# Twenty-four input-projection blocks as plain fp32 matmuls on a scaled copy of x

## The chip, the cores and the metric

The kernel runs on one core of a Trainium2 chip. The metric is the device time of one execution in microseconds (us). Three runs of the kernel before took 1295.62, 1296.11 and 1300.11 us, median 1296.11. Engines are named as in the profile: PE is TensorE (matmul; PEld its weight loads), DVE is VectorE, ACT is ScalarE, POOL is GpSimd, SP is SyncE, which here only issues DMAs.

## The reference

One encoder layer on 272 tokens (16 meta tokens and 256 of the input), width 2048, all in float32. RMSNorm of the input times `g` goes through one large projection W_in. Its columns are the input of an S5 state-space mixer (1024), queries and keys (1024), values (1024), output gates o (1024) and 32 gate values. Then two mixers run side by side, their outputs go through W_out, and a convolution-gated feed-forward part follows.

```
h  = h + W_out [ norm(S5(u)) || mLSTM(q, k, v, o, gates) ],   [u|qk|v|o|gates] = RMSNorm(h) W_in
h  = h + (silu(conv(hn W_gate)) * (hn W_up)) W_down,           hn = RMSNorm(h)
qk = silu(dwconv(qk_in));   y_ml = sigmoid(o_pre) * norm(mLSTM)
S5: y = gelu(scan_fwd(u) + scan_bwd(u) + d*u);  y * sigmoid(y W_glu + b)
```

## The kernel before

Activations stand with the channels on the 128 partitions and the 272 tokens along the free axis. Weights are streamed from DRAM in halves of 128x1024 (512 KB). A product has to be as good as float32: each half is split into a high part `hi` (ScalarE, L241) and a remainder `lo` (VectorE, L242) of the fast fp32r type, with three buffers each for `raw`, `hi` and `lo` (`piece`, from L236). `mm3` then does three matmuls per 128x128 weight tile (L257 to L259): hi times Xh, hi times Xl, lo times Xh, where Xh and Xl are x times g, split in the same way at the start (`split`, L279 and L280). A window block (`win_block`) is 128 columns of W_in: 16 weight tiles, two halves, 48 matmuls. There are 33 of them: one for the gate values, u0 to u7 for S5, qk0 to qk7 (of which qk0 to qk3 are the queries and need 258 columns only), v0 to v7, and o0 to o7 (258 columns). Each is emptied by VectorE, which multiplies by the token's factor R = 1/rms (L497, L638, L662, L681).

The S5 mixer has a chain of its own, on VectorE and GpSimd:
- tables of powers (`s5_tables`), of which one goes to DRAM (`td`, L375, two DMAs) and comes back spread over the partitions (`tcf`, L514);
- input coefficients for 16 half-blocks (L527 to L530), each followed by small matmuls, the in-projection (L543), into the state tile ST;
- a recurrence in three parts: `rec_local` (six steps of L551 to L554, first product on VectorE, second on GpSimd), `rec_carry` (15 steps of four small VectorE operations, L573 to L576), `rec_spread` (six steps in two halves, with the last sum on GpSimd);
- output coefficients for m = 0 to 7 (`s5_coefs`; zz L825 to L827 and c2 L834 on GpSimd, c1 L833 and L835 on VectorE), matmuls with them (L845, L860), a sum on VectorE that ends each m (L867), and a last matmul (L892);
- the GLU: a product with W_glu (L257 on `yg`) and a sigmoid (L925).

The mLSTM follows (L699 is one of its plain fp32 matmuls), then W_out and the feed-forward part.

The order of instructions on each engine is set when the program is built: a scheduler of the framework simulates the code and places each instruction where its simulated time and priority put it. `hp()` raises the priority of the code inside it; `behind` keeps one instruction behind another. In the code the blocks o, qk and v come after S5, but the scheduler puts them among S5's matmuls, where TensorE would wait. Tiles come from pools that stand at fixed places of SBUF on a left and a right side; a ring is a tag with a number of buffers that are used in turn.

Of the kernel before, what the change touches and what calls it, by code (L numbers as in the profile page):

```python
# [9 lines left out]
F32 = mybir.dt.float32  # L10
# [6 lines left out]
P = 128  # L17
# [4 lines left out]
KD = D // P  # L22
# [138 lines left out]
def body(ctx: ExitStack, tc: tile.TileContext, A: dict, out: bass.AP, dbg: dict = {}):  # L161
# [23 lines left out]
    def ring(p, tag, bufs):  # L185
        return lambda name, shape=(P, L), dt=F32: p.tile(list(shape), dt, tag=tag, bufs=bufs, name=name)

    l4 = ring(lq, "l4", 8)
    r1m = ring(lq, "r1m", 4)
    r1g = ring(lq, "r1g", 6)  # L190


    ST = ls.tile([P, 64, 2, C], F32, name="ST")
    STf = ST.rearrange("p a r c -> p (a r c)")
    e_li, li = pool("li")
    a4 = ring(li, "a4", 2)
    s2 = ring(li, "s2", 2)
# [94 lines left out]
    xcs = []  # L292

    def x_load(q, a=0, b=4):
        if a == 0:
            xcs.append(l4("xc", [P, 4, L]))
        return nc.sync.dma_start(xcs[q][:, a:b], A["xt"][:, 4 * q + a:4 * q + b, :])

    def x_split(q, a=0, b=4):
# [5 lines left out]
    def s5_tables():  # L305
# [66 lines left out]
            S.copy(tkc[0:64, 3 - i], t[0:64, :, 64:128])  # L372
            S.copy(tkc[64:128, i], t[64:128, :, 64:128])
        for d in range(2):
            nc.sync.dma_start(td[:, :, :, d].rearrange("s g j r p -> (g j) s (r p)"),  # L375
                              tkc[64 * d:64 * d + 64].rearrange("x s r p -> x s (r p)"))
        cmul(lam[2], l1, l1, 0, 64, G, w2, w3)
        cmul(lam[3], lam[2], l1, 0, 64, G, w2, w3)
# [42 lines left out]
    with hp():  # L421
        x_load(0, 0, 2)
        nc.sync.dma_start(vec, A["vec"])
        nc.sync.dma_start(par, A["par"])
        pieces = [piece(w0[:, :1024], CUTS)]
        x_split(0, 0, 2)
        x_load(0, 2)
        x_split(0, 2)
        x_load(1)
        x_split(1)  # L430
        pieces.append(piece(w0[:, 1024:], [1024]))
        for q in (2, 3):
            xd = x_load(q)
            x_split(q)
        get0 = getter(pieces)
        for q in range(4):
            S.activation(xcs[q], xcs[q], AF.Square)
            if q:
                (V if q == 3 else G).tensor_tensor(out=xcs[0], in0=xcs[0], in1=xcs[q], op=ALU.add)
# [3 lines left out]
    def X(t0, t1):  # L443
        return lambda i: (Xh[:, i, t0:t1], Xl[:, i, t0:t1])

    def win_block(b, t0=0):
        get = get0 if b == 0 else stream(A["win"][b], KD)
        p = bank("mm")
        mm3(p[:, :L - t0], get, X(t0, L), KD)
        return p  # L450

    pg = win_block(0)
    gsb = r1g("gsb")
    acc = bank("acc")
    tb = s5_tables()
    for j in range(4):
        nc.tensor.matmul(acc[:, :L], ones, xcs[0][:, j, :], start=(j == 0), stop=(j == 3))
    with hp():
        rstd(R, acc[:, :L], 1.0 / D)
    with hp():  # L460
# [5 lines left out]
    q_sb = l4("q_sb", [P, 4, N])
    kE = l4("kE", [P, 4, L])
    kO = l4("kO", [P, 4, L])
    osb = [l4("osb", [P, 4, N]) for _ in range(2)]
    for o in (*osb, q_sb):  # L470
        G.memset(o[:, 0, 0:1], 0.0)
    G.memset(kE[64:128], 0.0)
    G.memset(kO[0:64], 0.0)

# [153 lines left out]

    def qk_block(m):
        t0 = T0 if m < 4 else 0
        p = win_block(9 + m, t0)
        x = r1m("qx", [P, L + 2])
        G.memset(x[:, t0:t0 + 1], 0.0)
        G.memset(x[:, L + 1:L + 2], 0.0)
        with hp():
            V.tensor_tensor(out=x[:, t0 + 1:L + 1], in0=p[:, :L - t0], in1=R[:, t0:], op=ALU.mult)  # L638
        t = r1m("qt")
        tt = t[:, t0:]  # L640
        S.activation(tt, x[:, t0 + 1:L + 1], AF.Identity, scale=vc("qw", 8 + m), bias=vc("qb", m))
        with hp():
            V.scalar_tensor_tensor(out=tt, in0=x[:, t0:L], scalar=vc("qw", m), in1=tt, op0=ALU.mult, op1=ALU.add)
            V.scalar_tensor_tensor(out=tt, in0=x[:, t0 + 2:L + 2], scalar=vc("qw", 16 + m), in1=tt, op0=ALU.mult, op1=ALU.add)
        if m < 4:
            S.activation(q_sb[:, m, :], t[:, T0:], AF.Silu)
        else:
            S.activation(kE[0:64, m - 4, :], t[0:64], AF.Silu)
            S.activation(kO[64:128, m - 4, :], t[64:128], AF.Silu)

    Vt = [None, None, None]
    vm = lq.tile([P, 8, META], F32, name="vm")
    vmt = lq.tile([P, P], F32, name="vmt")

    def v_block(h):
        if h == 0:
            for i in range(3):
                Vt[i] = l4(f"V{i}", [P, 8, P])
        p = win_block(17 + h)
        vt = r1m("vt")  # L660
        with hp():
            V.tensor_tensor(out=vt, in0=p[:, :L], in1=R, op=ALU.mult)  # L662
# [284 lines left out]
    for m in range(8):  # L947
        u_block(m)
        if m < 4:
            behind(nc.sync.dma_start(bts[m], A["bt"][m]), last_raw[0])  # L950
        if m >= 1:
            s5_in(m - 1)
        if m == 4:
            G.memset(ST[:, 32:64, :, 0:1], 0.0)
    s5_in(7)
    rec_local(tb, 0)
    rec_local(tb, 1)
# [46 lines left out]
    nc.sync.dma_start(ch, A["cst"][:, NC0:])

# [135 lines left out]
```

## Time and profile before

| | us |
|---|---|
| median of three runs | 1296.11 |
| the profiled execution | 1294.34 |
| its span (first to last instruction) | 1292.6 |
| PE busy | 1225.7 (95%) |
| DVE busy | 874.2 (68%) |
| ACT busy | 603.8 (47%) |
| POOL busy | 369.6 (29%) |
| mean granted clock of TensorE | 0.972 |

Times in the rows below count from the span's start. A matmul's row gives its start and its length; matmuls overlap, so the distance from start to start is what one costs. A row "[2.49 <-DMA x]" says that the engine stood idle for 2.49 us before the instruction and what ended that. The parts of the program stand in the trace as follows: gate and u blocks up to 61 us, input coefficients to 115, `rec_local` to 176, `rec_carry` to 217, `rec_spread` to 273, output coefficients to 328, the last v blocks to 357, then the GLU.

### The profile page before, as it was taken

Reading aid. Unit: us, or ns where it says so; the run is one execution under the profiler, and the core shown is the slowest. Engines: PE = TensorE matmul, PEld = TensorE weight load, DVE = VectorE, ACT = ScalarE, POOL = GpSimd, SP = SyncE. Lnnn points to the kernel's source line nnn. Section 1 sums busy time; section 2 is a strip of 40 time slices with the busy share of each in tenths; the row PEclk is TensorE's granted clock in tenths of the full one; section 3 lists DMA queues with packets and bytes.
Section 4 is the critical chain, followed back from the end, with each engine's and each line's share of the span. In section 5 each row is a group of like instructions: output and inputs, shape, how many; then the busy total and the mean of one; then the engine's idle time right before and its main releaser. Section 6 shows DMA issues by size and latency. Waiting matters only on the chain.

```text
span 1292.6 us, 23440 instructions
## 1 busy us (share of the span) xinstructions
PE 1225.7 (95%) x9393; PEld 1126.8 (87%) x9393; DVE 874.2 (68%) x1083; ACT 603.8 (47%) x922; POOL 369.6 (29%) x428
## 2 busy tenths in 40 slices
PE   6889898898999999999999999999999999999995
PEld 5878898777998779999999998888999999998885
DVE  7779999973465488766666665555666666665554
ACT  7734244322476345544444444334444444445552
POOL 4476822685035363221111110000111111120111
PEclk8989899789999999999999999999999999999998
DMA  6777454343574355556556556666656656566663
GB/s 246 221 228 211 137 165 155 123 114 96 142 232 131 97 183 171 185 183 184 187 185 184 186 186 181 194 192 188 192 182 187 186 184 189 182 177 191 193 192 111
DMA packets 90753, 227.88 MB, mean 176 GB/s; under 512 B 21052, under 2 KB 36884, under 8 KB 90644
## 3 DMA queue, kind: packets, MB, share of 16 engines
q1 hardware_dynamic: 83924, 224.21, 57.0%
q10 hardware_dynamic: 6720, 2.16, 0.7%
q8 instruction: 74, 1.21, 0.4%
q14 instruction: 35, 0.29, 0.1%
HBM read 219.81 MB, written 5.48 MB: 174 GB/s over the span
## 4 chain that ended last, share of the span: by engine, by line
PE 75%; DVE 11%; DMA 4%; issue 4%; ACT 3%; POOL 1%; ACTq 1%; SPq 0%; DVEq 0%; POOLq 0%
PE ps_mm L268 25%; PE ps_mm L269 13%; PE ps_mm L257 10%; PE ps_mm L258 10%; PE ps_mm L259 10%; DVE lo L242 3%; PE ps_s L543 1%; ACTq L878 1%; DVE t L551 1%; PE ps_acc L845 1%; DVE ST L553 1%; PE ps_s L259 1%; PE ps_s L258 1%; PE ps_s L257 1%; ACT hi L241 1%
## 5 line engine op out<-in xcount | busy, mean ns | idle before, releaser
L242 DVE TENSOR_TENSOR lo<-raw,hi 128x1024 fp32r<-128x1024 f32 (+2 forms) x379 | 486.5, 1284 | 244.6 <-ACT hi L241 244.0
L241 ACT ACTIVATE hi<-raw 128x1024 fp32r<-128x1024 f32 (+2 forms) x379 | 393.8, 1039 | 461.0 <-PE ps_mm L268 202.4
L268 PE MATMUL ps_mm<-X,hi 128*128 128x512 f32 x704 | 249.8, 398 | 0.0
L268 PE MATMUL ps_mm<-a,hi 128*128 128x512 f32 x704 | 244.2, 390 | 0.0
L258 PE MATMUL ps_mm<-X,hi 128*128 128x258 f32 x704 | 199.6, 284 | 0.0
L1081 POOL TENSOR_TENSOR gt<-gt,R 128x256 f32<-128x256 f32 x44 | 59.5, 1352 | 487.1 <-ACT gt L1080 487.1
L257 PE MATMUL ps_mm<-X,hi 128*128 128x258 f32 x704 | 198.6, 282 | 0.0
L269 PE MATMUL ps_mm<-a,lo 128*128 128x256 f32 x704 | 198.5, 282 | 0.0
L259 PE MATMUL ps_mm<-X,lo 128*128 128x258 f32 x704 | 197.7, 281 | 0.0
L269 PE MATMUL ps_mm<-X,lo 128*128 128x256 f32 x704 | 197.0, 280 | 0.0
L259 PE MATMUL ps_mm<-Xh,lo 128*128 128x272 f32 (+1 forms) x528 | 161.9, 307 | 11.3 <-DVE lo L242 11.1
L257 PE MATMUL ps_mm<-Xh,hi 128*128 128x272 f32 (+1 forms) x528 | 160.5, 304 | 10.1 <-ACT hi L241 8.2
L258 PE MATMUL ps_mm<-Xl,hi 128*128 128x272 f32 (+1 forms) x528 | 159.2, 302 | 1.3 <-DVE Xl L280 1.3
L268 PEld LDWEIGHTS ps_mm<-X,hi 128*128 128x128 f32 x704 | 132.3, 188 | 29.5
L268 PEld LDWEIGHTS ps_mm<-a,hi 128*128 128x128 f32 x704 | 132.2, 188 | 27.7
L257 PEld LDWEIGHTS ps_mm<-X,hi 128*128 128x128 f32 x704 | 132.3, 188 | 2.2
L259 PEld LDWEIGHTS ps_mm<-X,lo 128*128 128x128 f32 x704 | 134.2, 191 | 0.0
L269 PEld LDWEIGHTS ps_mm<-X,lo 128*128 128x128 f32 x704 | 133.8, 190 | 0.0
L258 PEld LDWEIGHTS ps_mm<-X,hi 128*128 128x128 f32 x704 | 133.3, 189 | 0.0
L269 PEld LDWEIGHTS ps_mm<-a,lo 128*128 128x128 f32 x704 | 133.1, 189 | 0.0
L259 PEld LDWEIGHTS ps_mm<-Xh,lo 128*128 128x128 f32 x528 | 107.1, 203 | 15.2 <-DVE lo L242 14.0
L257 PEld LDWEIGHTS ps_mm<-Xh,hi 128*128 128x128 f32 x528 | 106.9, 203 | 12.3 <-ACT hi L241 8.5
(326 smaller groups left out, 1818.0 us busy)
## 6 DMA issues: line engine op xcount, KB each, us to landing
raw<-wg SPq DMA_DIRECT2D x88, 512.0 KB
raw<-wu SPq DMA_DIRECT2D x88, 512.0 KB, 4.4
raw<-win SPq DMA_DIRECT2D x65, 512.0 KB, 3.7
raw<-wd SPq DMA_DIRECT2D x64, 512.0 KB, 3.6
raw<-wout SPq DMA_DIRECT2D x32, 512.0 KB, 4.3
raw<-wd SPq DMA_DIRECT2D x32, 384.0 KB, 3.8
tcf<-td SPq DMA_DIRECT2D x16, 256.0 KB, 4.2
bc<-bcs SPq DMA_DIRECT2D x16, 256.0 KB, 3.4
```

The lines of the kernel that those rows point to most:

```text
L241: S.activation(hi[:, a:b], raw[:, a:b], AF.Copy)
L242: V.tensor_tensor(out=lo[:, a:b], in0=raw[:, a:b], in1=hi.bitcast(F32)[:, a:b], op=ALU.subtract)
L257: nc.tensor.matmul(out_ap, h, xh, start=(first and i == 0), stop=False)
L258: nc.tensor.matmul(out_ap, h, xl, start=False, stop=False)
L259: nc.tensor.matmul(out_ap, l, xh, start=False, stop=(last and i == n - 1))
L268: nc.tensor.matmul(both[:, :, :cols], h, x, start=(i == 0), stop=False)
L269: nc.tensor.matmul(both[:, 1, :cols], l, x[:, 0, :], start=False, stop=(i == n - 1))
L543: nc.tensor.matmul(pv[gg, d, ri, :], ic[gg, q, d, ri, :], uj[gg], start=True, stop=True)
L551: V.tensor_tensor(out=t1, in0=src, in1=lr[:, sl].unsqueeze(2).unsqueeze(3).to_broadcast([P, 32, 2, n]), op=ALU.mult)
L553: V.tensor_tensor(out=dst, in0=dst, in1=t1, op=ALU.add)
L845: mk_ = nc.tensor.matmul(kp[32 * g:32 * g + 32, 112 * qq + c0:112 * qq + c0 + 64], zf[gg, 16 * w:16 * w + 32], c1[gg, w].rearrange("p h k ...
L1081: G.tensor_tensor(out=t, in0=t, in1=R2[:, 2:], op=ALU.mult)
```

## The change

A new tile X holds x in float32 for the whole first part. After u0 VectorE multiplies it by g_mix and R in place, in 16 operations. The 24 blocks o, qk and v take their weights as they come from DRAM (`whole`) and multiply them as float32 with X (`win_plain`), one matmul call per weight tile where there were three. The three buffers of `raw`, `hi` and `lo` each serve in turn for such halves. Since R is in X already, ScalarE empties the blocks: the sigmoid of o is taken straight from PSUM, and `o_gates` goes away. The o and qk blocks use the PSUM banks of two tags in turn. The tiles osb, q_sb, kE, kO and V move to a pool of their own that opens where Xh and Xl end, the ring l4 goes from 8 buffers to 4 in another pool, the squares of x get tiles of their own, and h1 takes the place of X later. The S5 tables are built at high priority, and the two `td` stores are issued by ScalarE.

```diff
+    hx = ctx.enter_context(tc.tile_pool(name="hx", bufs=1, side="left"))
-    l4 = ring(lq, "l4", 8)
+    l4 = ring(ls, "l4", 4)
+    X = hx.tile([P, KD, L], F32, tag="h1", name="X")
+    xcs = [X[:, 4 * q:4 * q + 4, :] for q in range(4)]
...
-            nc.sync.dma_start(td[:, :, :, d].rearrange("s g j r p -> (g j) s (r p)"),
+            nc.scalar.dma_start(td[:, :, :, d].rearrange("s g j r p -> (g j) s (r p)"),
...
+    def whole(src):
+        tag = ("raw", "hi", "lo")[plain[0] % 3]
+        plain[0] += 1
+        w = st.tile([P, 1024], F32, tag=tag, bufs=3, name="wf")
+        nc.sync.dma_start(w, src)
+        return w
+
+    def win_plain(b, t0=0, tag="mm"):
+        p = bank(tag)
+        with hp():
+            w = [whole(A["win"][b][:, 1024 * j:1024 * j + 1024]) for j in range(2)]
+        for k in range(KD):
+            nc.tensor.matmul(p[:, :L - t0], w[k // 8][:, k % 8 * P:k % 8 * P + P], X[:, k, t0:],
+                             start=(k == 0), stop=(k == KD - 1))
+        return p
...
-    tb = s5_tables()
+    with hp():
+        tb = s5_tables()
...
-        p = win_block(9 + m, t0)
+        p = win_plain(9 + m, t0, ("mm", "ml")[m % 2])
-            V.tensor_tensor(out=x[:, t0 + 1:L + 1], in0=p[:, :L - t0], in1=R[:, t0:], op=ALU.mult)
-        S.activation(tt, x[:, t0 + 1:L + 1], AF.Identity, scale=vc("qw", 8 + m), bias=vc("qb", m))
+            S.copy(x[:, t0 + 1:L + 1], p[:, :L - t0])
+            S.activation(tt, p[:, :L - t0], AF.Identity, scale=vc("qw", 8 + m), bias=vc("qb", m))
...
-        p = win_block(17 + h)
+        p = win_plain(17 + h)
-            V.tensor_tensor(out=vt, in0=p[:, :L], in1=R, op=ALU.mult)
+            S.copy(vt, p[:, :L])
...
-        p = win_block(25 + h, T0)
-        o = osb[h // 4][:, h % 4, :]
-            V.tensor_tensor(out=o, in0=p[:, :N], in1=R[:, T0:], op=ALU.mult)
-    def o_gates():
-        for o in osb:
-            S.activation(o, o, AF.Sigmoid)
+        p = win_plain(25 + h, T0, ("mm", "ml")[h % 2])
+            S.activation(osb[h // 4][:, h % 4, :], p[:, :N], AF.Sigmoid)
...
+        if m == 0:
+            for k in range(KD):
+                V.scalar_tensor_tensor(out=X[:, k, :], in0=X[:, k, :], scalar=vc("g_mix", k), in1=R, op0=ALU.mult, op1=ALU.mult)
```

The change moves instructions in three places that matter below. The line numbers of the kernel after are up to 12 higher than those of the kernel before.

On SP before, the two stores of the table (td, from the tile tkc) stood among the loads of weight halves (raw):

```order
L375 DMA td<-tkc 64x4x128
L240 DMA raw<-win 128x1024
L375 DMA td<-tkc 64x4x128
L240 DMA raw<-win 128x1024
L624 DMA cmd<-gc 8x16 x2
L514 DMA tcf<-td 64x1x1024 x2
```

On ScalarE after, they stand among its hi parts and copies; un is the tile of a u block's columns:

```order
L242 ACTIVATE hi<-raw 128x1024
L514 COPY un<-un 128x4x16
L515 COPY un<-un 128x4x16
L373 COPY tkc<-ST 64x128
L374 COPY tkc<-ST 64x128
L376 DMA td<-tkc 64x4x128
L242 ACTIVATE hi<-raw 128x1024
L376 DMA td<-tkc 64x4x128
```

The second store now comes behind a hi, which is that of the second half of u5.

On VectorE before, at the start of the spread (t and ST are the recurrence's products and sums, qx and qt belong to the convolution of qk), lo parts stood between the steps:

```order
L242 TENSOR_TENSOR lo<-raw,hi 128x1024
L551 TENSOR_TENSOR t_1488<-ST,l4r 128x1024
L551 TENSOR_TENSOR t_1494<-ST,l8r 128x1024
L643 SCALAR_TENSOR_TENSOR qt<-qx,vec,qt 128x272
L553 TENSOR_TENSOR ST<-ST,t_1488 128x64x16
L242 TENSOR_TENSOR lo<-raw,hi 128x1024
L553 TENSOR_TENSOR ST<-ST,t_1494 128x64x16
L644 SCALAR_TENSOR_TENSOR qt<-qx,vec,qt 128x272
L638 TENSOR_TENSOR qx<-ps_mm,R 128x272
L242 TENSOR_TENSOR lo<-raw,hi 128x1024
L551 TENSOR_TENSOR t_1500<-ST,l12r 128x1024
```

On VectorE after, the same place:

```order
L562 TENSOR_TENSOR t_1513<-ST,l4r 128x1024
L562 TENSOR_TENSOR t_1519<-ST,l8r 128x1024
L564 TENSOR_TENSOR ST<-ST,t_1513 128x64x16
L564 TENSOR_TENSOR ST<-ST,t_1519 128x64x16
L562 TENSOR_TENSOR t_1525<-ST,l12r 128x1024
L564 TENSOR_TENSOR ST<-ST,t_1525 128x64x16
L562 TENSOR_TENSOR t_1531<-ST,l4r 128x1024
```

The steps follow each other, with no lo and no eviction between them.

On TensorE before, the matmuls of the output coefficients (ST times c, into ps_s) had matmuls of a v block on both sides, and others up to the end of S5:

```order
L257 MATMUL ps_mm<-Xh,hi 128x272
L860 MATMUL ps_s_1529<-ST,c_1536 64x68 x16
L860 MATMUL ps_s_1529<-ST,c_1579 64x68
L667 MATMUL ps_ml<-cst,vt 128x128 x2
L860 MATMUL ps_s_1529<-ST,c_1579 64x68 x15
L258 MATMUL ps_mm<-Xl,hi 128x272
L259 MATMUL ps_mm<-Xh,lo 128x272
```

On TensorE after, m = 0 stands inside qk2 (X times wf), m = 1 behind 7 matmuls of qk3:

```order
L467 MATMUL ps_mm<-X,wf 128x258 x13
L862 MATMUL ps_s_1554<-ST,c_1561 64x68 x16
L862 MATMUL ps_s_1554<-ST,c_1604 64x68 x16
L467 MATMUL ps_mm<-X,wf 128x258 x3
L467 MATMUL ps_ml<-X,wf 128x258 x7
L847 MATMUL ps_acc<-c_1652,zz 32x64 x8
L862 MATMUL ps_s_1645<-ST,c_1652 64x68 x8
```

and behind the last coefficients come the rest of qk3, qk4 to qk7 and all the v blocks (L674 are small matmuls of a v block that is done):

```order
L862 MATMUL ps_s_2284<-ST,c_2334 64x68 x8
L467 MATMUL ps_ml<-X,wf 128x258 x9
L467 MATMUL ps_mm<-X,wf 128x272 x13
L894 MATMUL ps_s_2170<-U,m_2382 64x68 x8
L894 MATMUL ps_s_2284<-U,m_2382 64x68 x8
L467 MATMUL ps_mm<-X,wf 128x272 x3
L467 MATMUL ps_ml<-X,wf 128x272 x16
L467 MATMUL ps_mm<-X,wf 128x272 x16
L467 MATMUL ps_ml<-X,wf 128x272 x16
L467 MATMUL ps_mm<-X,wf 128x272 x27
L674 MATMUL ps_ml<-cst,vt 128x128 x2
```

Between these two places no block matmul is left among the coefficients; before, 59 were.

## Rows read from the trace of the kernel before

**Rows 1.** Windows by stage: us, busy time (instructions), granted clock, DMA share, GB/s.
```profile
33.00:61.00 28.00, 26.08 (x198) 25.02 (x197) 21.43 (x37) 22.94 (x60) 11.46 (x25) 1.00 0.71 225
...
115.00:176.00 61.00, 55.44 (x533) 52.62 (x533) 60.93 (x48) 20.57 (x25) 43.58 (x27) 0.92 0.46 139
176.00:217.00 41.00, 41.00 (x339) 41.00 (x338) 40.66 (x92) 22.36 (x28) 1.36 (x11) 1.00 0.58 183
217.00:273.00 56.00, 44.53 (x388) 40.87 (x387) 53.75 (x40) 14.10 (x24) 42.09 (x19) 0.76 0.35 109
273.00:328.00 55.00, 50.34 (x918) 43.19 (x917) 21.72 (x31) 14.38 (x27) 29.64 (x44) 0.99 0.41 105
```

**Rows 2.** Groups by line: VectorE's L242 in 115 to 176, then 217 to 273.
```profile
L242 DVE TENSOR_TENSOR lo<-raw,hi 128x1024 fp32r<-128x1024 f32 x14 | 22.6, 1620 | 1.4 <-ACT hi L241 1.4
...
L242 DVE TENSOR_TENSOR lo<-raw,hi 128x1024 fp32r<-128x1024 f32 x10 | 16.0, 1596 | 0.0
```

**Rows 3.** Group by line: TensorE's L257 in 270 to 328.
```profile
L257 PE MATMUL ps_mm<-Xh,hi 128*128 128x272 f32 x20 | 6.5, 325 | 0.0
```

**Rows 4.** Timeline of TensorE, 35 steps apart: start us, length us, instruction.
```profile
254.06 0.29 PE L257 MATMUL ps_mm<-Xh,hi 128*128 128x272 f32 x1
...
258.45 0.29 PE L259 MATMUL ps_mm<-Xh,lo 128*128 128x272 f32 x1
```

**Rows 5.** Timeline, L699; then L457 by line (min/median/max ns; first, last start).
```profile
365.96 1.91 PE L699 MATMUL ps_ml<-q_sb,kM 128*128 128x258 f32 x8
...
L457 PE MATMUL ps_acc<-xc,ones x8: 392/392/393, 32.1 to 33.7; 128*128 128x272 f32 x8
```

**Rows 6.** Timelines of SP, TensorE and VectorE before the first S5 coefficients.
```profile
52.65 0.61 SPq L375 DMA_DIRECT2D td<-tkc  x1
...
57.37 0.29 PE L259 MATMUL ps_mm<-Xh,lo 128*128 128x272 f32 x1
...
62.41 2.36 DVE L527 TENSOR_TENSOR ic<-tcf,ST 128x512 f32<-128x512 f32 x2 [2.49 <-DMA tcf<-td]
```

**Rows 7.** VectorE's L280 (min/median/max ns, first and last start us, forms).
```profile
L280 DVE SCALAR_TENSOR_TENSOR Xl<-xc,vec,Xh x16: 483/496/2766, 6.1 to 23.6; 128x272 fp32r<-128x272 f32 x16
```

**Rows 8.** Timelines of VectorE and GpSimd, recurrence; then L554 and L552 by line.
```profile
114.02 1.58 DVE L242 TENSOR_TENSOR lo<-raw,hi 128x1024 fp32r<-128x1024 f32 x1 [1.37 <-ACT hi L241]
115.52 1.28 DVE L551 TENSOR_TENSOR t<-ST,l4r 128x1088 f32<-128x1088 f32 x1
...
176.00 0.37 DVE L573 TENSOR_TENSOR q<-ST,l16r 128x128 f32<-128x128 f32 x1
...
181.09 0.38 DVE L573 TENSOR_TENSOR q<-ST,l16r 128x128 f32<-128x128 f32 x1
...
182.53 0.39 DVE L573 TENSOR_TENSOR q<-ST,l16r 128x128 f32<-128x128 f32 x1
...
216.12 1.23 DVE L242 TENSOR_TENSOR lo<-raw,hi 128x1024 fp32r<-128x1024 f32 x1
217.26 3.05 DVE L551 TENSOR_TENSOR t<-ST,l4r 128x1024 f32<-128x1024 f32 x1
...
216.30 2.92 POOL L552 TENSOR_TENSOR t<-ST,l4i 128x1024 f32<-128x1024 f32 x1 [3.40 <-DVE ST L576]
...
270.10 2.80 POOL L554 TENSOR_TENSOR ST<-ST,t 128x1024 f32<-128x1024 f32 x1
...
L554 POOL TENSOR_TENSOR ST<-ST,t x6: 2497/2952/7043, 223.1 to 270.1; 128x1024 f32<-128x1024 f32 x6
...
L552 POOL TENSOR_TENSOR t<-ST,l8i x2: 2017/2499/2981, 226.0 to 256.6; 128x1024 f32<-128x1024 f32 x2
```

**Rows 9.** Timelines: VectorE's last L867, TensorE's first GLU matmul.
```profile
326.42 0.23 DVE L867 TENSOR_TENSOR ps_acc<-ps_acc,ed 64x64 f32<-64x64 f32 x1 [7.44 <-PE ps_acc L845]
...
356.56 0.29 PE L257 MATMUL ps_mm<-yg,hi 128*128 128x272 f32 x1
```

**Rows 10.** Timeline of ScalarE in the GLU.
```profile
362.91 1.28 ACT L738 ACT_TABLE_LOAD   x1
```

More of the change, by code (lines that the diff above doesn't have):

```diff
@@ L291, in body @@
     par = a4("par", [P, 3, P])
-    xcs = []
+    X = hx.tile([P, KD, L], F32, tag="h1", name="X")
+    xcs = [X[:, 4 * q:4 * q + 4, :] for q in range(4)]
     def x_load(q, a=0, b=4):
-        if a == 0:
-            xcs.append(l4("xc", [P, 4, L]))
         return nc.sync.dma_start(xcs[q][:, a:b], A["xt"][:, 4 * q + a:4 * q + b, :])
@@ L435, in body, with win_block @@
         get0 = getter(pieces)
+        sqs = [l4("sqx", [P, 4, L]) for _ in range(4)]
         for q in range(4):
-            S.activation(xcs[q], xcs[q], AF.Square)
+            S.activation(sqs[q], xcs[q], AF.Square)
             if q:
-                (V if q == 3 else G).tensor_tensor(out=xcs[0], in0=xcs[0], in1=xcs[q], op=ALU.add)
+                (V if q == 3 else G).tensor_tensor(out=sqs[0], in0=sqs[0], in1=sqs[q], op=ALU.add)
     behind(nc.sync.dma_start(cst, A["cst"][:, :NC0]), xd)
     bts = [STf[:, 64 * C + 1024 * i:64 * C + 1024 * i + 1024] for i in range(4)]
-    def X(t0, t1):
-        return lambda i: (Xh[:, i, t0:t1], Xl[:, i, t0:t1])
-    def win_block(b, t0=0):
+    def win_block(b):
         get = get0 if b == 0 else stream(A["win"][b], KD)
         p = bank("mm")
-        mm3(p[:, :L - t0], get, X(t0, L), KD)
+        mm3(p[:, :L], get, lambda i: (Xh[:, i, :], Xl[:, i, :]), KD)
+        return p
+    plain = [0]
+    def whole(src):
[11 more added lines that the diff above has]
+                             start=(k == 0), stop=(k == KD - 1))
         return p
@@ L454, in body @@
     acc = bank("acc")
-    tb = s5_tables()
+    with hp():
+        tb = s5_tables()
     for j in range(4):
-        nc.tensor.matmul(acc[:, :L], ones, xcs[0][:, j, :], start=(j == 0), stop=(j == 3))
+        nc.tensor.matmul(acc[:, :L], ones, sqs[0][:, j, :], start=(j == 0), stop=(j == 3))
     with hp():
@@ L463, in body @@
     dump("R", R)
[L466 to L473, printed above, removed]
     U = lq.tile([P, NP, UW], F32, name="U")
@@ L636, in qk_block @@
         G.memset(x[:, L + 1:L + 2], 0.0)
-        with hp():
-            V.tensor_tensor(out=x[:, t0 + 1:L + 1], in0=p[:, :L - t0], in1=R[:, t0:], op=ALU.mult)
         t = r1m("qt")
         tt = t[:, t0:]
-        S.activation(tt, x[:, t0 + 1:L + 1], AF.Identity, scale=vc("qw", 8 + m), bias=vc("qb", m))
+        with hp():
+            S.copy(x[:, t0 + 1:L + 1], p[:, :L - t0])
+            S.activation(tt, p[:, :L - t0], AF.Identity, scale=vc("qw", 8 + m), bias=vc("qb", m))
         with hp():
@@ L649, in qk_block @@
             S.activation(kO[64:128, m - 4, :], t[64:128], AF.Silu)
-    Vt = [None, None, None]
     vm = lq.tile([P, 8, META], F32, name="vm")
@@ L655, in v_block @@
     def v_block(h):
-        if h == 0:
-            for i in range(3):
-                Vt[i] = l4(f"V{i}", [P, 8, P])
-        p = win_block(17 + h)
+        p = win_plain(17 + h)
         vt = r1m("vt")
         with hp():
-            V.tensor_tensor(out=vt, in0=p[:, :L], in1=R, op=ALU.mult)
+            S.copy(vt, p[:, :L])
         with hp():
@@ L954, in body @@
             G.memset(ST[:, 32:64, :, 0:1], 0.0)
+    e_rx.close()
+    e_qk, qk = pool("qk", "right")
+    q_sb = qk.tile([P, 4, N], F32, name="q_sb")
+    kE = qk.tile([P, 4, L], F32, name="kE")
+    kO = qk.tile([P, 4, L], F32, name="kO")
+    osb = [qk.tile([P, 4, N], F32, name=f"osb{i}") for i in range(2)]
+    Vt = [qk.tile([P, 8, P], F32, name=f"V{i}") for i in range(3)]
+    G.memset(q_sb[:, 0, 0:1], 0.0)
+    G.memset(kE[64:128], 0.0)
+    G.memset(kO[0:64], 0.0)
     s5_in(7)
@@ L994, in body @@
         v_block(h)
-    e_rx.close()
-    e_rh, rh = pool("rh", "right")
-    h1 = rh.tile([P, KD, N], F32, name="h1")
+    h1 = hx.tile([P, KD, N], F32, tag="h1", name="h1")
     e_hs, hs = pool("hs", "right")
@@ L1001, in body @@
     s5_glu()
-    o_gates()
     ch = hs.tile([P, NCST - NC0], F32, name="ch")
@@ L1033, in body @@
     e_hs.close()
+    e_qk.close()
     ym = ml["y"]
@@ L1124, in body @@
     e_rh2.close()
-    e_rh.close()
 def kernel(**inputs):
```

## Prediction

> **What bounds the kernel now.** First the table of busy shares: TensorE is busy 95% of the span, so a change of its work counts wherever it does not wait. Next the windows by stage [rows 1], because the change touches only what lies ahead of the S5 output gate (GLU), whose first matmul stands at 356.56 us [rows 9]. There the share hides two regimes. From 115 to 273 us TensorE follows VectorE: VectorE is busy 60.93 of 61 us in the local recurrence (115 to 176), 40.66 of 41 in the carry (176 to 217) and 53.75 of 56 in the spread (217 to 273). In the spread TensorE is busy 44.53 of 56 us at a granted clock of 0.76 on average. From 273 on VectorE is free (21.72 of 55) and TensorE is the limit (50.34 of 55). The input-projection blocks are split by ScalarE and VectorE into hi and lo halves. In the stretches where VectorE is full, 14 and 10 of its instructions are such lo halves: 22.6 and 16.0 us [rows 2]. So before 273 us the change takes work from the bound engine, and behind it adds work to the engine that bounds there. I set the two against each other at the first GLU matmul.
>
> **What it adds on TensorE.** Three fp32r matmuls per weight tile make 48 in a block. At full clock a step of 272 columns takes (258.45 - 254.06)/35 = 0.1254 us, a block 6.02. With 258 columns it is 258/272 of that, 5.71 [rows 4]. A plain fp32 matmul counts as two records here. Eight records of 128x258, whose weights change, take 1.91 us at one record's 0.381: (1.91 - 0.38)/7 = 0.218, so 32 records are 6.99 us a block. With 272 columns eight records start between 32.1 and 33.7 us, 0.2286 apart: 7.31 us a block [rows 5]. Twelve blocks of each width: 12 x (6.99 - 5.71) + 12 x (7.31 - 6.02) = +30.8 us. The 1.91 us row excludes that the weight loads come on top of that pitch. I take the durations at the upper clock level, at which 273 to 328 ran (0.99) [rows 1], for all of them.
>
> **What it takes away and moves, stage by stage.** All times are on the clock of the profiled execution.
> - Start of the S5 coefficients. VectorE's first product, L527, starts at 62.41, set free by the table that went to DRAM with two stores on SP, the second at 52.65 [rows 6]. Now the stores stand on ScalarE, the second behind the hi of block u5's second half. That hi needs a buffer that TensorE frees with u4's first half, whose last matmul starts at 57.37 [rows 6]. The 16 scalings of x (0.496 us each, by an operation of the same form and size [rows 7]) stand between u1's and u2's lo on VectorE. Of their 8 us, 33 to 61 has 28 - 21.43 = 6.6 us of idle VectorE [rows 1], so they cost TensorE 2 to 6 us, and I take 4. Then the store goes out at about 62.5 (57.4 + 4, and 1 for the hi itself) instead of 52.65, and L527 starts at **72.4 (+10)**. Bounds: +4 (the hi comes free as it did) to +14.
> - Input coefficients, to the first local step (62.41 to 115.52 [rows 6, 8]): 53.1 us, but the wait of 1.37 and the lo just ahead of it go, 50.25. Six more lo leave at 1.15 (from start to next start: 216.12 to 217.26 is 1.14 [rows 8]): 43.3. TensorE now reaches the first in-projection inside u7, about 1 us late: 44.3, to **116.7**.
> - Local recurrence (115.52 to 176.00, 60.5 us): 13 lo at 1.15 (15 us) and 7 evictions at 0.33 go: 43.2, to **159.9**. GpSimd's own part there was 43.58 us [rows 1], and its order is as before. That is why I don't go lower.
> - Carry: 15 steps. A step without a lo is 182.53 - 181.09 = 1.44 us [rows 8]: 21.6, and 2.5 for what stands between, to **184.0**.
> - Spread (217.26 to 270.10 + 2.80 = 272.9 [rows 8], 55.6): 9 lo (10.3), convolutions and evictions (3), the first c1 products (4.5) and, on GpSimd, the c2 and zz products of m=2 (3.3) no longer stand in it: 34.5, to **218.5**. On GpSimd alone the spread's 12 products add up to some 33 us: six L554 of 2.95 in the median and six L552 of 2.5 [rows 8]. So 30 is about the floor.
> - Output coefficients m=2 to 7: before, from 272.9 to the last sum L867 at 326.42 [rows 9], 53.5 us. TensorE's 59 block matmuls between them (20 each of L257 and L259 and 19 of L258 [rows 3]; 59 x 0.1254 = 7.4) now stand elsewhere, while m=2's products come behind the spread (+2) and TensorE has waited before it (half clock at the start, +2): 50, to **268.5**. Bounds 46 and 56.
> - The tail. Before, 356.56 - 326.42 = 30.1 us. Now the static order puts 9 matmuls of qk3 and 12 whole blocks behind the coefficients: 9 x 0.436 + 12 x 7.31 = 91.6, and 2.5 for two small matmuls per v block and the last S5 output: 94, to **362.5**.
>
> TensorE comes to the first coefficients of m=0 at about 180 to 185 and waits there for the spread's first half, at about 206. That wait of some 20 us is what the shorter chain does not give back, since 12 blocks are held behind the coefficients and not put into it.
>
> The sum: 362.5 - 356.6 = +5.9. In the GLU one sigmoid is late now behind a table load at 362.91 for the first head's exponentials [rows 10]; in the new order these stand earlier: -2. Together **+3.9 us**. Nothing behind is touched that the order shows late. On the profiled execution that is 1294.3 + 3.9 = 1298.2, and the median of the runs is 1.8 us above it (1296.11 against 1294.34): **1300.0 us**. A measurement here can tell about 0.5%, 6.5 us, from no change.
>
> **A rule weighed.** The first spread product on VectorE took 3.05 us beside GpSimd's 2.92, where the lo of the same size just ahead of it took 1.23; it ends 1.09 us after GpSimd's [rows 8]. So it hardly moved while the other ran. The Trainium skill (SBUF — State Buffer, "Who interferes with whom") says that the two share a port pair under an exclusive lock, and that the loser waits until it is free. By this row the rule holds; by the stages it is not the whole, since the shortest instance of each kind of product in 115 to 176 gives an estimate of 46 us on VectorE (32 long ones at 1.2 and some 7 of the rest) and 24 on GpSimd. In turns that is about 70, and 60.5 elapsed.
>
> **Rivals.**
> 1. *The two engines take turns* (slower). With the lo gone, what is left on VectorE meets GpSimd more often: every step is one product on each. If they exclude each other wholly, the local part is the same estimate without lo and evictions, 70 - 14 x 1.21 - 7 x 0.4 = 50 instead of 43.2; the spread is 12 products of VectorE at 1.14 from start to start and GpSimd's, at their shortest (2.5 and 2.0) 27: 40.7 instead of 34.5; the input part loses 2: +15, so about **1315**. For it: the 3.05 us row. Against it: 60.5 elapsed where turns would need 70. By the skill's rule above this would be the outcome. It decides the sign once the chain loses over 3 us more than I allow.
> 2. *The lo cost more than 1.15* (faster). In the two stages they take 22.6/14 = 1.61 and 16.0/10 = 1.60 on average [rows 2], since they too wait for GpSimd. If all of that comes back: 13 x 0.46 + 9 x 0.45 = 10.0; the coefficients at their lower bound of 46 give 4, and a table that comes 4 us earlier 4: 1300 - 18 = **1282**. For it: VectorE is at 100% there. Against: GpSimd's 43.58 and some 33 us are nearly as long as my stages already. TensorE's 20 us of waiting is the room for it.
> 3. *Nothing comes of the shorter chain*: the wait at m=0 moves with the table and what TensorE gains is eaten by a lower clock. Then only +30.8 - 2 stays: **1325**.
>
> **How the numbers follow.** Forecast (1293 to 1308 as its own range, from the bounds of the start, -6, and of the coefficients, +6 either way) 0.57; rival 1 0.13; rival 2 0.25; rival 3 0.05. Range: 1282 to 1317. Faster by over 6.5 us (under 1289.6): rival 2 and a little of the forecast, 0.28. Within: most of the forecast, 0.35. Slower: the rest of the forecast, rivals 1 and 3, 0.37.
>
> **What would show it.** The first L527 near 72; local about 43, carry about 24, spread about 35 us; a wait of TensorE of 15 to 25 us at m=0's matmuls with the clock low behind it; the last L867 near 268; then twelve blocks in a row of 7.31 us, and the first GLU matmul near 362. The forecast is wrong if a block takes over 7.4 us at full clock, if the table comes as early as before, or if the chain ends before 255 or after 282.

## The result and the profile after

The changed kernel takes 1328.97 us (median of four runs, 1326.23 to 1330.18) beside 1296.50 of the kernel before: 1.0242 times as long, 95% interval 1.0216 to 1.0268. (The 1296.50 is the median of the three runs named above and a fourth.) Forecast were 1300.0 us, 1282 to 1317. The profiled execution took 1330.18 us, its span 1328.3, the mean granted clock 0.968.

The windows of the kernel after, in other cuts than those of before, with the columns of [rows 1]:

```profile
150.00:190.00 40.00, 37.66 (x220) 32.89 (x219) 37.00 (x69) 4.07 (x8) 21.53 (x16) 0.96 0.43 136
190.00:230.00 40.00, 19.69 (x133) 16.79 (x131) 39.69 (x22) 2.32 (x7) 32.99 (x16) 0.78 0.15 48
230.00:270.00 40.00, 32.86 (x594) 28.32 (x596) 17.61 (x25) 8.00 (x14) 23.13 (x36) 0.80 0.39 108
270.00:310.00 40.00, 35.00 (x487) 29.55 (x487) 8.50 (x16) 9.90 (x22) 9.29 (x20) 0.91 0.38 103
310.00:350.00 40.00, 40.00 (x178) 33.14 (x177) 6.98 (x14) 18.99 (x40) 2.99 (x14) 1.00 0.51 157
350.00:390.00 40.00, 40.00 (x183) 33.09 (x181) 2.46 (x2) 8.51 (x25) 0.00 (x0) 1.00 0.31 106
```

TensorE is busy 19.69 of 40 us in the spread (190 to 230) and 67.86 of 80 among the output coefficients (230 to 310), at a granted clock of 0.78 to 0.91. From 310 us on it is busy without a gap. The waits of TensorE up to 390 us (us in all, times, longest) say why:

```profile
PE ps_s L862 <- POOL ST L565: 16.5, 1, 16.5
PE ps_mm L258 <- ACT hi L242: 9.9, 2, 7.1
PE ps_s L894 <- ACT m L888: 9.9, 4, 3.6
PE ps_mm L260 <- DVE lo L243: 5.7, 3, 4.1
PE ps_s L554 <- DVE ic L540: 5.2, 4, 2.8
PE ps_acc L847 <- DVE c L837: 4.4, 1, 4.4
```

One wait of 16.5 us stands at m=0, where TensorE's order wants the first half of the spread. Four waits stand at L894, the last matmul of a pair of m, which needs `m`, a copy of what eight small DMAs have moved.

The rows on the timelines that answer to those of [rows 6, 8, 9]; names of lines are those of the kernel after:

```profile
62.40 0.59 ACTq L376 DMA_DIRECT2D td<-tkc  x1
...
74.10 1.78 DVE L538 TENSOR_TENSOR ic<-tcf,ST 128x512 f32<-128x512 f32 x1
...
123.62 1.28 DVE L562 TENSOR_TENSOR t<-ST,l4r 128x1088 f32<-128x1088 f32 x1
...
169.54 0.39 DVE L584 TENSOR_TENSOR q<-ST,l16r 128x128 f32<-128x128 f32 x1
...
191.39 1.23 DVE L562 TENSOR_TENSOR t<-ST,l4r 128x1024 f32<-128x1024 f32 x1
...
226.83 2.41 POOL L565 TENSOR_TENSOR ST<-ST,t 128x1024 f32<-128x1024 f32 x1
...
237.80 0.23 DVE L869 TENSOR_TENSOR ps_acc<-ps_acc,ed 64x64 f32<-64x64 f32 x1 [1.14 <-PE ps_acc L847]
...
295.07 0.22 DVE L869 TENSOR_TENSOR ps_acc<-ps_acc,ed 64x64 f32<-64x64 f32 x1 [9.08 <-PE ps_acc L847]
...
391.17 0.49 PE L258 MATMUL ps_mm<-yg,hi 128*128 128x272 f32 x1
```

From these rows, with the end of one stage as the start of the next (us):

| step | before | forecast | after |
|---|---|---|---|
| first input coefficient at | 62.4 | 72.4 | 74.1 |
| input part, to the first local step | 53.1 | 44.3 | 49.5 |
| local recurrence | 60.5 | 43.2 | 45.9 |
| carry | 41.3 | 24.1 | 21.9 |
| spread | 55.6 | 34.5 | 37.8 |
| from the spread to the last sum of the coefficients | 53.5 | 50 | 65.8 |
| from there to the first GLU matmul | 30.1 | 94 | 96.1 |
| first GLU matmul at | 356.6 | 362.5 | 391.2 |

The chain on VectorE did get shorter: its last sum stands at 295 instead of 326. But TensorE has 96 us of work behind it where it had 30. From the first GLU matmul to the end of the span it is 937.1 us after (1328.3 - 391.2) and 936.0 before: the rest of the kernel takes as long as it did.

### The profile page after: what moved, and what is told of

The parts are those of the page before. It is cut to its first block, busy times and chain, and to the rows that moved or that the text cites. A ratio compares the mean times of both kernels' runs of the same rounds, so it can differ in the third digit from the quotient of the medians.

```text
span 1328.3 us, 22498 instructions
## 1 busy us (share of the span) xinstructions
PE 1248.3 (94%) x9009; PEld 1124.5 (85%) x9009; DVE 817.7 (62%) x1027; ACT 565.9 (43%) x900; POOL 352.0 (27%) x426
## 3 DMA queue, kind: packets, MB, share of 16 engines
q8 instruction: 71, 1.16, 0.4%
## 4 chain that ended last, share of the span: by engine, by line
PE 74%; DVE 11%; DMA 7%; ACT 2%; POOL 2%; issue 2%; ACTq 2%; DVEq 0%; SPq 0%; POOLq 0%
PE ps_mm L269 24%; PE ps_mm L270 13%; PE ps_mm L258 8%; PE ps_mm L259 8%; PE ps_mm L260 8%; PE ps_mm L467 5%; PE ps_ml L467 2%; ACTq L880 1%; DVE t L562 1%; DVE lo L243 1%; DMA raw<-win 1%; DVE ST L564 1%; DMA U<-yd 1%; DMA bcf<-bt 1%; DMA ms<-gx 1%
## 5 line engine op out<-in xcount | busy, mean ns | idle before, releaser
L243 DVE TENSOR_TENSOR lo<-raw,hi 128x1024 fp32r<-128x1024 f32 (+2 forms) x331 | 416.1, 1257 | 290.7 <-ACT hi L242 234.9
L242 ACT ACTIVATE hi<-raw 128x1024 fp32r<-128x1024 f32 (+2 forms) x331 | 342.8, 1036 | 409.8 <-PE ps_mm L269 194.7
L467 PE MATMUL ps_mm<-X,wf 128*128 128x272 f32 (+1 forms) x512 | 121.3, 392 | 0.0
L467 PEld LDWEIGHTS ps_mm<-X,wf 128*128 128x128 f32 x512 | 96.4, 191 | 17.6
L467 PE MATMUL ps_ml<-X,wf 128*128 128x258 f32 (+1 forms) x256 | 62.9, 399 | 0.0
L467 PEld LDWEIGHTS ps_ml<-X,wf 128*128 128x128 f32 x256 | 49.1, 195 | 8.7 <-issue 0.2
L258 PE MATMUL ps_mm<-Xh,hi 128*128 128x272 f32 x144 | 45.7, 317 | 10.0 <-ACT hi L242 9.9
```

The source lines that it names most:

```text
L242: S.activation(hi[:, a:b], raw[:, a:b], AF.Copy)
L243: V.tensor_tensor(out=lo[:, a:b], in0=raw[:, a:b], in1=hi.bitcast(F32)[:, a:b], op=ALU.subtract)
L258: nc.tensor.matmul(out_ap, h, xh, start=(first and i == 0), stop=False)
L467: nc.tensor.matmul(p[:, :L - t0], w[k // 8][:, k % 8 * P:k % 8 * P + P], X[:, k, t0:], start=(k == 0), stop=(k == KD - 1))
```

## The experiments

The result and the experiments come from four series of runs. The kernel before was run in each: 1296.50 us (with the kernel after), then 1297.78, 1298.04 and 1299.36. So 3 us between runs of different series say nothing. The edits are shown abridged.

**TensorE's order.** The first experiment leaves every operation as it is and writes blocks ahead of the output coefficients in the code, so that the scheduler prefers them:

```diff
     pos, last = [], None
+    for h in range(8):
+        o_block(h)
+    late = [qk0 .. qk7, v0 .. v7]        # as calls
+    for _ in range(6):
+        late.pop(0)()
     for m in range(8):
+        if m: late.pop(0)()
         po, m0 = s5_coefs(m, tb)
...
-    (the three loops over o_block, qk_block, v_block)
+    for f in late: f()
```

> The kernel after, with the blocks o0 to o7 and qk0 to qk5 written ahead of the output coefficients and the ten others between them, one per m. Nothing is left out. Theory (the time is lost because TensorE stands without block matmuls: from 200 to 300 us it is busy 68.5 of 100, and 13 of its 24 blocks come behind the last coefficient): TensorE's wait at m=0 and the waits and low clock among the coefficients are filled, first GLU matmul at 355 to 368 instead of 391, time 1293 to 1308 us. Rival 1 (the S5 chain, which starts 12 us late, sets the end wherever the blocks stand): 1320 to 1330. Rival 2 (the four-pass blocks cost so much on TensorE that their sum sets the time): 1325 to 1335.

Measured: 1300.54 us, first GLU matmul at 362.03, ratio to before 1.0023 (1.0013 to 1.0032). So 28 of the 32 us were lost to the order and not to the price of the blocks. The S5 chain up to the spread's end hardly moved (228.4 against 229.2). The rival by which the chain sets the end falls, and so does the one by which the sum of the blocks' work does.

A wait was left there. Timeline of ScalarE in this run:

```profile
214.04 0.42 ACT L657 ACTIVATE q_sb<-qt 128x258 f32<-128x258 f32 x1 [32.59 <-DVE qt L655]
214.36 0.36 ACT L651 COPY qx<-ps_ml 128x258 f32<-128x258 f32 x1
```

and TensorE's:

```profile
199.98 7.50 PE L467 MATMUL ps_mm<-X,wf 128*128 128x272 f32 x32
215.24 9.89 PE L467 MATMUL ps_ml<-X,wf 128*128 128x272 f32 x32 [7.76 <-ACT qt L652]
```

ScalarE stood 32.6 us at a silu that wanted a convolution step of VectorE, which in turn stood behind the spread. The copies that empty the next qk blocks were queued behind it, TensorE waited 7.76 us for a PSUM bank, and the next block ran in 9.89 us instead of 7.50: the granted clock is 0.51 up to 220.00 us and 1.00 behind it, so about half of these 10 us ran at the lower level.

**o and v ahead, qk between the coefficients.** The v blocks need no VectorE, so they go first:

```diff
-    late = [qk0 .. qk7, v0 .. v7]
+    late = [v0 .. v7, qk0 .. qk7]
```

> As the first experiment, but o and six v blocks stand ahead of the coefficients, and two v and the eight qk blocks between them. There ScalarE stood 32.6 us at a silu that waited for a convolution step of VectorE in the spread, so a PSUM bank was not emptied, TensorE waited 7.8 us and ran 10 us at half clock. Theory (that head-of-line wait costs the time): it goes, as v needs no VectorE; 8 to 12 us less than 1300.5, 1288 to 1293. Rival (TensorE only waits elsewhere, for the spread): 1298 to 1303.

Measured: 1286.87 us (1286.41 to 1287.53), ratio to before 0.9920 (0.9896 to 0.9944), 1 us under the expected range. It is 42 us faster than the kernel after and 11 us faster than the kernel before beside it (1298.04): 0.8%, small, but clear of the spread of the runs. Its windows:

```profile
150.00:190.00 40.00, 40.00 (x182) 34.07 (x181) 38.72 (x71) 3.16 (x10) 16.65 (x10) 1.00 0.51 171
190.00:230.00 40.00, 40.00 (x277) 32.59 (x276) 39.22 (x19) 5.06 (x19) 36.70 (x15) 1.00 0.34 106
230.00:270.00 40.00, 39.64 (x497) 32.07 (x497) 10.95 (x17) 10.20 (x22) 20.21 (x34) 1.00 0.49 147
270.00:310.00 40.00, 40.00 (x492) 33.42 (x492) 10.88 (x19) 10.75 (x19) 13.41 (x26) 1.00 0.47 133
310.00:350.00 40.00, 40.00 (x346) 33.16 (x346) 11.12 (x20) 23.30 (x47) 5.14 (x18) 1.00 0.37 101
```

From 150 to 350 us TensorE is idle for 0.4 us in all, and the granted clock is 1.00 (2.4 GHz, the upper level). In this stretch its own work sets the pace, up to the first GLU matmul at 349.26.

**Which of the two places.** The next two are edits of the version with o and v first. One has blocks ahead of m=0 only (none among the coefficients), the other among the coefficients only (as many ahead of m=0 as in the kernel after, o0 to o7 and not quite three more):

```diff
-        if m: late.pop(0)()
+        (left out)
```

> As the one with o and v first (1286.9 us), but without block matmuls among the output coefficients: six v blocks stand ahead of m=0, the ten other blocks behind m=7. Theory (both places count: the 16.5 us wait at m=0 and the waits for DMAs and ScalarE among the coefficients): the first place alone gives back about half of the 41 us between the kernel after and the one with o and v first; TensorE waits among the coefficients as in the kernel after (3 us at each L894, half clock behind them): last L869 at 290 to 297, first GLU matmul 366 to 372, time 1303 to 1309. Rival (the wait at m=0 is all): 1287 to 1291.

```diff
-    for _ in range(6):
+    for _ in range(0):
```

> The other half: ahead of m=0 stand as many block matmuls as in the kernel after (114), and blocks stand between the coefficients from m=2 on. Theory (both places count): TensorE waits 13 to 17 us at m=0 as in the kernel after, and hardly at the L894; time 1305 to 1315. Rival (the wait at m=0 costs nothing, since the coefficients are bound by their own chain): 1287 to 1295.

Measured: 1305.84 us ahead only, 1319.96 between only; the kernel after 1328.97, both together 1286.87. So 23 us come from the first place alone and 9 from the second alone, and both together give 42: the parts don't add. Read the other way: with the first place filled, filling the second as well gives another 19 us (1305.84 to 1286.87). In the first run the waits among the coefficients stand as they were:

```profile
PE ps_s L894 <- ACT m L888: 11.2, 4, 3.5
```

The second missed its range by 5 us. TensorE waits there 12.7 us at m=0, and 10.2 at the transposes of v blocks (waiting for ScalarE's emptying of the block); 190 to 230 is 21.62 of 40 busy at 0.70. Since v blocks stand there where qk blocks stood, its order differs from the kernel after in more than was meant, and it sizes the second place less well than the first run sizes the first.

**All eight v ahead**, again as an edit of the version with o and v first:

```diff
-    for _ in range(6):
+    for _ in range(8):
```

> As the one with o and v first, with all eight v blocks ahead of the coefficients. Theory (TensorE is without gaps from 150 us on in the kernel with six, so that the sum of its work sets the time): nothing is won or lost, 1285 to 1289. Rival (two blocks more ahead push the coefficients' chain back, which then ends last): 1292 to 1300.

Measured: 1303.73 us, 17 more than with six. The rival was right in kind, and its range was 4 us short. The last sum of the coefficients comes at 340.51 instead of 325.1, and then TensorE has only one block left to cover the last DMA, copy and gelu. Waits of TensorE from 330 to 390:

```profile
PE ps_ml L467 <- ACT cT L631: 5.1, 1, 5.1
PE ps_mm L258 <- ACT yg L912: 4.6, 1, 4.6
PE ps_mm L258 <- ACT sg L927: 2.3, 1, 2.3
```

The windows 310 to 350 and 350 to 390 have clocks of 0.93 and 0.86. The three waits add up to 12 of the 17 us; the rest is probably the lower clock, which was not tested. So some blocks have to stay behind the coefficients too: three are enough in the version with o and v first, one is too few, and the twelve and a half of the kernel after are too many.

**The same order in the kernel before**, with its three-pass blocks:

> The kernel before with the same order in the code as in the first experiment (o and six qk blocks ahead of the output coefficients, the others between them); its blocks are three-pass. Nothing is left out. Theory (the order pays only where the blocks need no VectorE): VectorE is full from 115 to 273 us already, so the lo of more blocks in that stretch push the S5 chain back, spread end at 285 or later, time 1296 to 1315. Rival (the order gains by itself, so that the before kernel would gain the same 25 to 30 us): 1268 to 1280.

Measured: 1300.71 us, ratio 1.0027 (1.0013 to 1.0042): no gain. The time lies in the expected range, but not by the expected way: the spread ends at 272.6, as before, and was not pushed back. VectorE's lo parts up to 273 us, in this run and in the kernel before:

```profile
L242 DVE TENSOR_TENSOR lo<-raw,hi x59: 423/1215/3070, 7.6 to 269.2; 128x1024 fp32r<-128x1024 f32 x57, 128x256 fp32r<-128x256 f32 x1, 128x768 fp32r<-128x768 f32 x1
...
L242 DVE TENSOR_TENSOR lo<-raw,hi x59: 418/1224/3067, 7.7 to 267.0; 128x1024 fp32r<-128x1024 f32 x57, 128x256 fp32r<-128x256 f32 x1, 128x768 fp32r<-128x768 f32 x1
```

It is 59 in both: the order in the code brought no block half forward. That VectorE, full up to 273 us, is what holds them is argued from this and was not tested. With the same order in the code the four corners are 1296.50 us (neither change), 1300.71 (order alone), 1328.97 (plain blocks alone) and 1300.54 (both): the order gives back 28 us with plain blocks and nothing with three-pass blocks. The order that beats the kernel before, o and v first, was not run with three-pass blocks, so what the plain blocks add to it is not shown.

**The price of the blocks in the tail.** The v blocks multiply only half of their weight tiles (the rest of the sum is left out):

```diff
-        for k in range(KD):
+        kn = 8 if 17 <= b < 25 else KD
+        for k in range(kn):
```

> The kernel after with the v blocks multiplying only the first 8 of their 16 weight tiles (the rest of the sum is left out; both halves of the weights are still loaded). TensorE's order up to the last coefficient is the same. Theory (the tail behind the coefficients is TensorE's four-pass time alone): 8 x 16 records x 0.2286 = 29 us less, 1298 to 1303 us. Rival (the tail waits for the weights or for ScalarE emptying the blocks): under 20 us less, 1309 to 1320.

Measured: 1302.48 us, 26.5 less than the kernel after, first GLU matmul at 363.68 instead of 391.17: 27.5. Expected were 29: the tail is TensorE's time, as forecast, but for some 2 us. In the kernel after, 32 records of 272 columns start at 331.16 and end where the next block starts:

```profile
331.16 0.62 PE L467 MATMUL ps_mm<-X,wf 128*128 128x272 f32 x2
...
338.04 0.85 PE L467 MATMUL ps_mm<-X,wf 128*128 128x272 f32 x3
```

The last of these three is the next block's first, at 338.50: 7.34 us, where 7.31 were forecast from the mLSTM's and the norm's plain matmuls [rows 5].

**The start of the chain.** The stores back on SyncE, first in the kernel after, then in the version with o and v first:

```diff
-            nc.scalar.dma_start(td[:, :, :, d]...
+            nc.sync.dma_start(td[:, :, :, d]...
```

> The kernel after with the two table stores issued by SyncE again, TensorE's order being unchanged. Theory (blocks behind the coefficients, chain on the critical path): the chain starts earlier only by what ScalarE's queue held back, 0 to 3 us, since the copies before the store are themselves late (61.2): time 1325 to 1330. Rival (the move of the store is what delays the chain by 10 us): first input coefficient at 64 to 66 and time 1317 to 1321.

> As the one with o and v first, with the table stores on SyncE. Theory (TensorE is the limit, and the store was held back by its copies and not by the queue): 1285 to 1288. Rival (the chain's start still counts): 1281 to 1284.

Measured: 1326.76 and 1287.51 us, against 1328.97 and 1286.87. The two differences lie within the 3 us between series. The queue is not the cause: the first input coefficient comes at 74.48 with SyncE and at 74.10 with ScalarE. The copy that makes the table is itself late. ScalarE in the kernel after:

```profile
61.24 0.30 ACT L373 COPY tkc<-ST 64x128 f32<-64x128 f32 x1 [1.25 <-DVE ST L363]
61.57 0.29 ACT L374 COPY tkc<-ST 64x128 f32<-64x128 f32 x1
61.58 0.70 ACTq L376 DMA_DIRECT2D td<-tkc  x1
```

It waits for the table's products on VectorE. Without the 16 multiplications of x (left out):

```diff
-            for k in range(KD):
-                V.scalar_tensor_tensor(out=X[:, k, :], ...)
```

> The kernel after without the 16 multiplications of x by g_mix and R (that part of the computation is left out). Theory: VectorE gets 8 us earlier to the tables and to the lo of u1 and u2, and the in-projection stands among the u blocks again; the first input coefficient comes at 64 to 68 instead of 74, and all behind it as much earlier: 1318 to 1323 us. Rival (the scalings are hidden, the store's queue is the cause): no change, 1326 to 1331.

Measured: 1323.05 us. The first input coefficient comes at 57.33, 17 us earlier, twice as much as the 8 us of the operations (expected were 64 to 68). Only 7 us of it arrive at the GLU (384.19): in this order the in-projection stands among the u blocks again, whose lo VectorE has to make, and input part and local recurrence take 52.3 and 52.2 us. With the multiplications kept, but behind u4:

```diff
-        if m == 0:
+        if m == 4:
             for k in range(KD):
-                V.scalar_tensor_tensor(out=X[:, k, :], ...)
+                behind(V.scalar_tensor_tensor(out=X[:, k, :], ...), last emptying of a u block)
```

This edit is made in the version with o and v first.

> As the one with o and v first, and the 16 multiplications of x stand on VectorE behind the emptying of u4. Theory: the tables and u2's lo are 8 us earlier, the first input coefficient at 57 to 62; as TensorE is the limit now, only its early waits (for hi and lo of u2, 4 to 6 us) come back: 1283 to 1289. Rival (the S5 chain still bounds): 8 to 12 us less, 1278 to 1282; or the in-projection among the u blocks takes it back: no change.

Measured: 1292.47 us, 5.6 slower than with the multiplications early; slower than anything expected. The first input coefficient comes at 58.92, but the local recurrence starts at 122.50 (123.53 with the multiplications early), almost as if nothing had come earlier, and TensorE is busy 32.34 of 38 us from 62 to 100, where it was 34.68. Where the 5.6 us come from was not followed further.

**The weight buffers.** Unsplit halves in the three raw buffers alone:

```diff
-        tag = ("raw", "hi", "lo")[plain[0] % 3]
+        tag = "raw"
```

> The kernel after, whose unsplit weight halves use the three raw buffers alone and not all nine. Theory (the input part took 49.5 us, 5 more than forecast, because nine halves fetched ahead, with the DMAs busy 0.96 from 61 to 100 us, hold back the tables tcf and bcf): the DMA waits of the first coefficients go, local recurrence starts at 118 to 121 instead of 123.6, time 1323 to 1327. Rival (the part is long because TensorE comes late to the in-projection, behind u6): no change before 123, 1327 to 1332, or slower where TensorE waits for weights.

Measured: 1333.82 us, local recurrence at 124.56, no earlier than 123.62. The DMAs' share from 62 to 100 us fell from 0.96 in the kernel after to 0.81 here, without a gain. VectorE's waits for DMAs in the input part fell from 8.9 us to 2.4, but what it waited for TensorE's in-projection (L554) rose by more; the kernel after, then this run:

```profile
DVE ic L538 <- PE ps_s L554: 11.5, 6, 3.2
...
DVE ic L538 <- PE ps_s L554: 21.8, 8, 5.3
```

That the input part is long because of crowded DMAs is refuted.

## Why the prediction was wrong, by its steps

*The price of the blocks* was right: 7.34 us measured for 7.31, and the tail 96.1 for 94. The first GLU matmul came 28.7 us later than forecast (391.2 for 362.5).

*The order* was read rightly: TensorE waited 16.5 us at m=0, forecast were about 20, and the twelve blocks stood behind the coefficients. What I did not ask is what these blocks did for TensorE before, besides taking its time.

*The step that failed is the output coefficients*, 50 us forecast with 46 and 56 as bounds, and 65.8 measured: 15.8 of the 28.7 us. The sign that the prediction named came, too: the chain ended after 282, at 295.07. TensorE's windows from the spread's end and from sum to sum, before (m=2, then m=3 and 4, m=5 and 6, m=7):

```profile
272.90:281.70 8.80, 8.80 (x143) 7.47 (x143) 3.31 (x5) 1.69 (x5) 7.55 (x11) 0.94 0.44 96
281.70:299.85 18.15, 18.15 (x309) 15.81 (x311) 9.86 (x12) 4.87 (x7) 11.16 (x16) 1.00 0.55 150
299.85:316.83 16.98, 14.17 (x294) 12.01 (x294) 6.71 (x10) 4.39 (x10) 9.50 (x17) 1.00 0.36 94
316.83:326.42 9.59, 7.75 (x166) 6.49 (x166) 1.72 (x3) 2.31 (x5) 1.52 (x3) 1.00 0.26 66
```

and after (m=1, then the pairs m=2 and 3, m=4 and 5, m=6 and 7):

```profile
229.24:237.80 8.56, 7.15 (x116) 6.08 (x118) 6.24 (x9) 0.42 (x1) 4.99 (x8) 0.60 0.47 143
237.80:256.45 18.65, 15.74 (x294) 13.57 (x296) 6.77 (x10) 4.56 (x8) 10.45 (x17) 0.82 0.38 104
256.45:275.19 18.74, 15.16 (x294) 13.02 (x294) 6.82 (x10) 3.02 (x6) 10.30 (x17) 0.91 0.37 98
275.19:295.07 19.88, 15.83 (x294) 13.58 (x293) 4.99 (x9) 3.41 (x7) 5.85 (x12) 0.83 0.22 52
```

Two things were missed. First, m=1. Before, its sum came at 270.6, ahead of the spread's end at 272.9; now it comes at 237.80, 8.6 us behind the end at 229.24, after a wait of 4.4 us for its c1 and at a granted clock of 0.60. The forecast took its c1 products out of the spread (-4.5) and put nothing in behind it; the +2 there was for m=2's products.

Second, m=2 to 7: 57.3 us, 3.8 more than before, although no block matmul stands in it any more. The forecast had taken 7.4 us out for 59 of them. That reading was too high: the window of [rows 3] is wider than the stage, in which 41 of the 59 stand, 5.1 us. And what left did not shorten the stage, because TensorE waits at the end of each pair of m, for eight DMAs and a copy. Its idle time from m=2 to 7 grew from 4.7 to 10.5 us. TensorE in the kernel after, at the first two of these places:

```profile
247.62 2.08 PE L894 MATMUL ps_s<-U,m 64*64 64x68 f32 x32 [2.91 <-ACT m L888]
...
266.88 2.08 PE L894 MATMUL ps_s<-U,m 64*64 64x68 f32 x32 [3.58 <-ACT m L888]
```

In the kernel before, at the second and the third:

```profile
301.94 1.17 PE L892 MATMUL ps_s<-U,m 64*64 64x68 f32 x32 [1.58 <-ACT m L886]
...
319.18 1.16 PE L892 MATMUL ps_s<-U,m 64*64 64x68 f32 x32 [1.84 <-ACT m L886]
```

At the first place before, 285.09 us, there was no wait: 27 block matmuls stood just ahead of it, from 281.53 on. At the other two no block matmul stood ahead, and the waits were shorter than after all the same, so covered waits are not the whole account. The same 32 matmuls take 2.08 us instead of 1.16, at the lower level of the clock (windows of the first such place after, and of the second before):

```profile
247.62:249.70 2.08, 2.08 (x34) 1.95 (x36) 0.00 (x0) 0.76 (x2) 0.05 (x1) 0.50 0.08 25
...
301.94:303.04 1.10, 1.10 (x33) 1.02 (x33) 0.24 (x1) 0.74 (x2) 0.78 (x1) 1.00 0.48 95
```

So the 15.8 us are 8.6 for m=1 and 7.3 for m=2 to 7. By these rows 5.9 us more of waiting and, as an estimate, 3 us of lower clock (busy 46.7 us after, against 48.9 less the 5.1 of the blocks) stand against the 4 us that the forecast had allowed; the rest is the 7.4 that was 5.1. This split is read from the rows, not tested. That filling these places gives time back is shown by the experiments on the two places.

*The input part*, 49.5 for 44.3: DVE's waits for TensorE (11.5 us at L538 for the in-projection, L554, where it was 5.4) point to TensorE's coming late, behind u6. With the three buffers VectorE waited less for DMAs and more for TensorE (21.8 us), and the part got no shorter. That the place of the in-projection is the cause was not tested by itself, and the late multiplications, which moved it, gained nothing.

*The start*: the size was right (+11.7 for +10), and the mechanism half wrong. I put 4 us on the multiplications and the rest on the queue behind the hi. The runs show that the queue costs nothing and that without the multiplications the table comes 17 us earlier.

*The spread and the local part*, 37.8 for 34.5 and 45.9 for 43.2, lie between the sum and the full exclusion of rival 1 (40.7 and 50). The forecast for the spread is near what GpSimd needs for its own twelve products, 33 us in the kernel after; what it took beyond these is GpSimd's waits for VectorE's L564, 4.7 us (1.2, 1.2 and 2.4). The forecast had also taken the convolution out of the spread, and four steps of it still stand there (L654 and L655, 7.0 us of VectorE); but in the version with o and v first none does, and its spread is 37.6 us too. Under the exclusive lock of which the Trainium skill speaks (SBUF — State Buffer, "Who interferes with whom") the two engines would take turns. By these times they don't wholly, and what the lock costs was not measured by itself. *The carry* was 2.2 us shorter.

*The term of -2 us for the sigmoid in the GLU* was right in its wait (TensorE waited 2.3 us for it before and 0.4 after) and did not show in the time: from the first GLU matmul to the end it is 937.1 us for 936.0.

*The rivals*: the time was nearest to the third's 1325, to which I gave 0.05, but not by its way. By that rival nothing comes of the shorter chain, because a lower clock eats it. But the chain's last sum came 31 us earlier, and what ate this was the order, whose gaps brought a lower clock with them. The second rival's mechanism, lo that cost more than 1.15, did not show. What I should have had is a rival that the filler is missing among the coefficients, and a wider view of the wait at m=0: a wait of some 20 us that I had seen in the order was the place where a version could win, and I booked it as a fixed cost.

## What to carry to other kernels

Work taken off a full engine shortens its chain; whether the time follows depends on where the released engine's own work stands in the order. When a change makes filler work independent of the bound engine, move that filler into the waits, and leave enough of it for the last ones: o and six v blocks ahead gave 1286.9 us, o and all eight v 1303.7, and the kernel after, with o and not quite three qk blocks ahead and none among the coefficients, 1329.0. Before forecasting that a stage gets shorter because other work leaves it, ask which waits that work covered.

## What was not expected of the hardware

In these rows a gap of a few us on TensorE cost more than itself: behind waits of 2.91 and 3.58 us the next 32 small matmuls took 2.08 us (granted clock 0.50, 1.2 GHz), behind waits of 1.58 and 1.84 us 1.17 and 1.16 (granted clock 1.00, 2.4 GHz). From 190 to 230 and from 230 to 270 us the granted clock is 0.78 and 0.80 in the kernel after, and 1.00 in the same windows when the gaps are filled.
